# An encoder trunk on one core: the second sum of a seven-product pair in its own tile, one unit's copies dealt out, and two constants rebuilt later

## The chip, the cores and the metric

The kernel runs on one core of one Trainium2 chip. Its time is the device time of one execution, in microseconds. The core has a tensor engine (PE), a vector engine (DVE), a scalar engine (ACT), GpSimd (POOL) and SyncE (SP). Each works through its own queue of instructions in order and waits on semaphores; transfers are issued from the queues of SP, POOL and ACT.

## The reference

Two residual layers on x of 256 tokens by 2048 features, all in float32. The first layer's mixer is grouped-query attention, the second's a recurrent block; each is followed by a gated feed-forward layer.

```python
D_MODEL = 2048; SEQ = 256; DEPTH = 2
D_FF = 5632

def swiglu(h, w_gate, w_up, w_down):
    return (jax.nn.silu(h @ w_gate) * (h @ w_up)) @ w_down

def reference(x, ...):
    for i in range(DEPTH):
        h = rms_norm(x, norm_mix[i])
        mix = attention_mixer(h, ...) if i % N_MIXERS == 0 else recurrent_mixer(h, ...)
        x = x + mix
        x = x + swiglu(rms_norm(x, norm_ffn[i]), ffn_w_gate[i], ffn_w_up[i], ffn_w_down[i])
    return x
```

## The kernel before

**Products.** Every float32 operand is split in two parts that PE can multiply fast: hi, a cast of the value by ACT, and lo, the value less hi, by DVE (here called the correction). One product of a 128x128 block of x with 128x512 weights is three matmuls (`product`, L323, L324, L326): hi by hi, lo by hi, hi by lo.

**Feed-forward layer.** 5632 hidden features are eleven units of 512 (`unit`). A unit multiplies all of x (two token blocks) with 512 columns of the gate and 512 of the up matrix. The 2048 features of x are eight pairs of blocks, numbered 0 to 7. A pair comes in two forms:

- With eight products (`wide`): the gate half and the up half are loaded, 128x1024 each, cast by ACT (L145) and corrected by DVE (L146).
- With seven products (`load_seven`, after Strassen): the weights b11, b21, t1, b22 come in two landing buffers (raw), and further operands are formed: t1 = b11 + t1 (by DVE, L174, if the three loads before were of eight-product pairs, otherwise by an adding transfer on POOL, L176), then t2 = t1 + b22, t3 = t2 - b11, t4 = b21 + t2 (L169, DVE). Each is cast (L163 for the two whole buffers, L170 for t2, t3 and t4) and corrected (L164, L171). PE takes them in the order b11, b21, t1, b22, t2, t3, t4.

`SEVEN` and `FEWER` say which pairs have seven products: six of the eight (0, 1, 2, 4, 5, 6) in most units, fewer in the first three: 0, 5, 6 in the first, 4, 5, 6 in the second, 1, 4, 5, 6 in the third (the code's units 0, 1, 2).

At the end of a unit, from its pair 7 on, DVE and ACT put the products together (`sums`, L769 to L773, and L791, L794), apply SiLU, multiply gate by up (L795), and turn the result from tokens to features: DVE transposes 32x32 blocks (L408), sixteen copies put them in place (L416, in four moves of four), and L801 and L802 split the result into hi and lo. If `beside` is set, the four moves are put into a list (`tail`), and the next unit's seven-product pairs take one each; the last is followed by L801 and L802. `beside` is set for all units but the first and the last. The first unit's sixteen copies are issued at once, on ACT.

After the third unit come down projections, two groups behind each unit.

**Buffers.** Loads land in eight buffers during a feed-forward layer (five of a standing pool, three of the layer's own pool), and hi and lo go to seven pairs of buffers; t2's hi and lo have two of their own. t2 was written over b22, in the second landing buffer, so it had to wait until b22 was cast and corrected, and the buffer was held until t2 was corrected.

**Order.** PE executes in the order in which the program is written. A scheduler sets the order on the other engines, by times that it estimates and by rules in the code: `behind` keeps all casts in their written order on ACT, and all corrections and sums in theirs on DVE.

**Before the recurrent layer.** When the first feed-forward layer's pool is closed, the recurrent layer's pool ("rp") opens in its place. The norm's factors, one a token, are needed as a row (`Norm.spread`, due 26 steps later): DVE multiplies ident, the unit matrix, by them (dg, L492), PE multiplies ones by dg (L493), ACT copies the row (L495), and the convolution uses it (L842). ones and ident stand in a pool that lasts for the whole program; ident is loaded at the start, from in_cn_dram.

Of the kernel before, what the change touches and what calls it, by code (L numbers as in the profile page):

```python
# [12 lines left out]
F32 = mybir.dt.float32  # L13
F32R = mybir.dt.float32r
AF = mybir.ActivationFunctionType
ALU = mybir.AluOpType
AX = mybir.AxisListType

P = 128
S = 256  # L20
# [7 lines left out]
PARTS = [8, 8, 8, 8, 12]  # L28
UNIT = 4
SEVEN = (0, 1, 2, 4, 5, 6)  # L30
FEWER = {0: (0, 5, 6), 1: (4, 5, 6), 2: (1, 4, 5, 6)}
HALF = 8
CHUNK = HALF * P
WIDE = 512
# [40 lines left out]
def trunk(ctx, tc, w, out):  # L75
# [17 lines left out]
    def tmp(tag, shape=(P, S), dt=F32, bufs=2):  # L93
        pl = tp if tag in COMMON else scope[-1]
        return pl.tile(list(shape), dt, tag=tag, name=nm(tag), bufs=bufs)
# [58 lines left out]
    def load_seven(srcs, soon):  # L154
        raw = [landing([P, 2, WIDE]) for _ in range(2)]
        for r, src in zip(raw, srcs):
            sync.dma_start(out=r, in_=src)
        (b11, b21), (t1, b22) = ([r[:, j, :] for j in range(2)] for r in raw)
        got = {}

        def two(src, names):
            hi, lo = parts([P, 2, WIDE])
            behind("cast", act.copy(hi, src))  # L163
            behind("rest", dve.tensor_tensor(lo, src, hi[:].bitcast(F32), ALU.subtract))  # L164
            for j, name in enumerate(names):
                got[name] = hi[:, j, :], lo[:, j, :]

        def combine(o, x, y, op, hi, lo):
            behind("rest", dve.tensor_tensor(o, x, y, op))  # L169
            behind("cast", act.copy(hi, o))  # L170
            return lambda: behind("rest", dve.tensor_tensor(lo, o, hi.bitcast(F32), ALU.subtract))  # L171

        if soon:
            behind("rest", dve.tensor_tensor(t1, b11, t1, ALU.add))  # L174
        else:
            pool.dma_start(out=t1, in_=b11, accum_op=ALU.add)  # L176
        two(raw[0], ("b11", "b21"))
        two(raw[1], ("t1", "b22"))
        if tail:
            tail.pop(0)()  # L180
        one = [tmp(t, (P, WIDE), F32R) for t in ("ohi", "olo")]
        hi, lo = parts([P, 2, WIDE])
        got["t2"] = tuple(one)
        got["t3"], got["t4"] = ((hi[:, j, :], lo[:, j, :]) for j in range(2))
        t2 = b22
        rests = [
            combine(t2, t1, b22, ALU.add, *got["t2"]),
            combine(b11, t2, b11, ALU.subtract, *got["t3"]),
            combine(b21, t2, b21, ALU.add, *got["t4"]),
        ]  # L190
        while parted:
            follow(parted.pop(), newest["cast"])
        for rest in rests:
            rest()
        return got
# [71 lines left out]
    def later(delay, fn):  # L267
        waiting.append((clock[0] + delay, fn))
# [113 lines left out]


    x_tm = cst.tile([P, 2, D], F32, tag="x", name="x")
    ident = cst.tile([P, P], F32, tag="ident", name="ident")
    pk = cst.tile([P, PKW], F32, tag="pk", name="pk")
    at = ctx.enter_context(ExitStack())
    ap = at.enter_context(tc.tile_pool(name="ap", bufs=2))
    scope.append(ap)
    xq = [ap.tile([P, 4, S], F32, tag=f"xq{k}", name=f"xq{k}", bufs=1) for k in range(KT // 4)]  # L390
    cn = ap.tile([P, 2 * S], F32, tag="cn", name="cn", bufs=1)
    ones = cst.tile([P, P], F32, tag="ones", name="ones")
    act.dma_start(out=pk[:, :PK0], in_=w["pk"][:, :PK0])
    pool.memset(ones, 1.0)
    idle = ps_m.tile([P, P], F32, tag="pm", name=nm("pm"))
# [354 lines left out]
    def ffn(norm, nxt):  # L750
# [60 lines left out]
        ends = np.cumsum(PARTS) // UNIT  # L811
        for what, i in ffn_plan():
            if what == "unit":
                hid[int(np.searchsorted(ends, i, "right"))] += unit(FEWER.get(i, SEVEN), 0 < i < ends[-1] - 1, (act,) if i < ends[-1] - 1 else (act, dve), i < ends[0])
            else:
                for a, acc in enumerate(wide_project(hid[i[0]], PARTS[i[0]], bank)):
                    t = tmp("form", (P, WIDE))
# [14 lines left out]

    rt = ctx.enter_context(ExitStack())
    scope.append(rt.enter_context(tc.tile_pool(name="rp", bufs=2)))
    later(SPREAD, nr.spread)

    def conv_branch(ct, bank, first=False):
# [205 lines left out]
```

## Time and profile before

| | |
|---|---|
| time, median of 3 runs | 1952.84 us (1952.83 to 1952.92) |
| the profiled execution's own time | 1952.89 us |
| its span, first to last instruction | 1951.1 us |
| granted clock of PE | 1.000 |
| busy: PE / DVE / ACT / POOL | 1938.0 / 1768.6 / 1448.3 / 401.3 us |
| first feed-forward layer | about 266 to 950 us of the span |
| recurrent layer begins | about 950 us |

A row of the timeline gives start and length in us, engine, line, operation, out<-in and shape; in brackets the idle time of the engine before it and what ended it. Matmuls overlap, so their lengths (0.39) are longer than the distance of their starts (0.227). L123 is line 123 of the kernel before; in the changed kernel some lines are moved by one to three.

### The profile page before, as it was taken

To read this page: it belongs to the slowest core of one execution; us is meant where nothing else is said; L and a number is where in the kernel's file an instruction comes from. 1 tells how busy PE (TensorE), PEld (TensorE's weight loads), DVE (VectorE), ACT (ScalarE), POOL (GpSimd) and SP (SyncE) were. 2 spreads that over 40 slices of the span, in tenths; PEclk is the share of its full clock that TensorE was granted. 3 is DMA by queue.
4 is the path that set the end of the run, shared out by engine and by line. 5 is a ranking of instruction groups with operands and counts; after the bars stand their busy time and mean duration, and the time that the engine had idled before them with its cause. 6 is when DMAs were issued, how large, how long until landed. Compare 5 with 4: busy or idle time off the path is not lost.

```text
span 1951.1 us, 27630 instructions
## 1 busy us (share of the span) xinstructions
PE 1938.0 (99%) x9224; PEld 1624.0 (83%) x9224; DVE 1768.6 (91%) x2417; ACT 1448.3 (74%) x2358; POOL 401.3 (21%) x497
## 2 busy tenths in 40 slices
PE   9999999999999999999999999999999999999999
PEld 8898888788888888888899998887888888888887
DVE  7878698999999999998799997898999999999993
ACT  7677686777777777777698887866778776787772
POOL 0442250011101111010465450520101111011100
PEclk9999999999999999999999999999999999999999
DMA  8434746698878978787365556555878888788872
GB/s 328 156 127 152 248 158 197 196 272 236 248 233 243 262 240 246 235 244 246 126 223 188 189 164 245 175 194 174 253 236 248 245 248 253 231 246 251 246 257 86
DMA packets 131727, 426.42 MB, mean 219 GB/s; under 512 B 14720, under 2 KB 14976, under 8 KB 131584
## 3 DMA queue, kind: packets, MB, share of 16 engines
q1 hardware_dynamic: 108944, 383.21, 58.0%
q0 software_dynamic: 22496, 41.43, 11.9%
q8 instruction: 72, 1.18, 0.2%
q14 instruction: 71, 0.58, 0.1%
q10 hardware_dynamic: 144, 0.02, 0.0%
HBM read 382.13 MB, written 2.10 MB: 197 GB/s over the span
## 4 chain that ended last, share of the span: by engine, by line
PE 92%; DVE 4%; ACT 1%; issue 1%; DMA 1%; POOL 0%; SPq 0%; ACTq 0%; DVEq 0%; POOLq 0%
PE acc L326 14%; PE acc L323 14%; PE acc L324 14%; PE pm L326 11%; PE pm L323 11%; PE pm L324 11%; PE acc L294 8%; PE acc L292 4%; PE pm L306 1%; PE pm L307 1%; PE pm L305 1%; DVE lo L146 1%; ACT hi L145 1%; DVE lo L164 0%; DMA raw<-in_w_in_dram 0%
## 5 line engine op out<-in xcount | busy, mean ns | idle before, releaser
L146 DVE TENSOR_TENSOR lo<-raw,hi 128x1024 fp32r<-128x1024 f32 (+1 forms) x474 | 574.5, 1240 | 77.1 <-ACT hi L145 75.3
L145 ACT CAST hi<-raw 128x1024 fp32r<-128x1024 f32 (+1 forms) x474 | 478.4, 1045 | 116.5 <-PE acc L324 72.1
L326 PE MATMUL acc<-lo,xg 128*128 128x512 f32 x744 | 290.9, 391 | 2.0 <-DVE lo L146 1.8
L323 PE MATMUL acc<-hi,xg 128*128 128x512 f32 x744 | 290.0, 390 | 0.0
L324 PE MATMUL acc<-hi,xg 128*128 128x512 f32 x744 | 289.6, 389 | 0.0
L164 DVE TENSOR_TENSOR lo<-raw,hi 128x1024 fp32r<-128x1024 f32 x232 | 275.0, 1217 | 6.5 <-ACT hi L163 3.8
L294 PE MATMUL acc<-xg,hi 128*128 128x512 f32 x832 | 271.7, 397 | 0.6 <-ACT hi L145 0.6
L163 ACT CAST hi<-raw 128x1024 fp32r<-128x1024 f32 x232 | 234.6, 1048 | 41.0 <-issue 14.4
L176 POOL DMA_DIRECT2D raw<-raw x90 | 77.7, 863 | 903.9 <-DVE raw L174 369.5
L323 PE MATMUL pm<-hi,act 128*128 128x512 f32 x512 | 199.2, 389 | 0.0
L324 PE MATMUL pm<-hi,act 128*128 128x512 f32 x512 | 199.2, 389 | 0.0
L326 PE MATMUL pm<-lo,act 128*128 128x512 f32 x512 | 199.2, 389 | 0.0
L416 ACT COPY two<-one 32x256 f32<-32x256 f32 x420 | 169.7, 404 | 24.7 <-DVE one L408 16.5
L292 PEld LDWEIGHTS acc<-xg,lo 128*128 128x128 f32 x832 | 156.3, 188 | 35.4 <-DVE lo L146 2.8
L323 PE MATMUL acc<-hi,act 128*128 128x512 f32 x448 | 174.9, 390 | 0.4 <-DVE two L794 0.4
L326 PE MATMUL acc<-lo,act 128*128 128x512 f32 x448 | 174.4, 389 | 0.0
L324 PE MATMUL acc<-hi,act 128*128 128x512 f32 x448 | 174.4, 389 | 0.0
L292 PE MATMUL acc<-xg,lo 128*128 128x256 f32 x832 | 171.8, 281 | 1.2 <-DVE lo L146 1.2
L326 PEld LDWEIGHTS acc<-lo,xg 128*128 128x128 f32 x744 | 139.7, 188 | 34.1 <-DVE lo L146 5.4
L324 PEld LDWEIGHTS acc<-hi,xg 128*128 128x128 f32 x744 | 139.7, 188 | 29.2
L323 PEld LDWEIGHTS acc<-hi,xg 128*128 128x128 f32 x744 | 139.7, 188 | 28.6
L170 ACT CAST hi<-raw 128x512 fp32r<-128x512 f32 x232 | 137.1, 622 | 32.8 <-DVE raw L169 31.8
(221 smaller groups left out, 3852.1 us busy)
## 6 DMA issues: line engine op xcount, KB each, us to landing
raw<-in_w_gate_dram SPq DMA_DIRECT2D x176, 512.0 KB, 4.6
raw<-in_w_up_dram SPq DMA_DIRECT2D x176, 512.0 KB, 5.5
raw<-in_w_down_dram SPq DMA_DIRECT2D x176, 512.0 KB, 4.4
raw<-in_w_in_dram SPq DMA_DIRECT2D x64, 512.0 KB, 4.4
raw<-raw POOLq DMA_DIRECT2D x90, 256.0 KB, 5.8
raw<-in_w_q_dram SPq DMA_DIRECT2D x32, 512.0 KB, 3.8
raw<-in_w_o_dram SPq DMA_DIRECT2D x32, 512.0 KB, 4.2
x<-form POOLq DMA_DIRECT2D x64, 256.0 KB, 6.7
```

Source lines behind the costliest of these rows:

```text
L145: behind("cast", act.copy(hi[:, sl], raw[:, sl]))
L146: behind("rest", dve.tensor_tensor(lo[:, sl], raw[:, sl], hi[:, sl].bitcast(F32), ALU.subtract))
L163: behind("cast", act.copy(hi, src))
L164: behind("rest", dve.tensor_tensor(lo, src, hi[:].bitcast(F32), ALU.subtract))
L170: behind("cast", act.copy(hi, o))
L176: pool.dma_start(out=t1, in_=b11, accum_op=ALU.add)
L292: pe.matmul(acc[:, S:], w, xs[k][:, :S], start=False, stop=stop)
L294: pe.matmul(acc, w, xs[k], start=(k == 0), stop=stop)
L323: pe.matmul(o, xh, wh, start=start, stop=False)
L324: pe.matmul(o, xl, wh, start=False, stop=False)
L326: pe.matmul(o, xh, wl, start=False, stop=stop)
L416: m = (eng.copy if eng is act else eng.tensor_copy)(to[:, :, :, i, :], of[:, :, :, j, :])
```

## The change

1. t2 gets a tile of its own (`sum`, one buffer). Its sum is issued ahead of the casting and correcting of the second landing buffer on DVE, and its cast ahead of the move of copies that the pair takes from the list. t3 and t4 are formed, cast and corrected as before, their casts behind the copies.
2. `beside` is set for the first unit too: its copies are dealt out over the second unit's seven-product pairs, which are four now.
3. The second unit's pairs with seven products become 2, 4, 5, 6 (three before), the third's 2, 4, 5, 6 in place of 1, 4, 5, 6.
4. ones and ident leave the pool that lasts for the whole program. They are built in the attention layer's pool, and again in the recurrent layer's pool, by a memset and a transfer on POOL.

```diff
-FEWER = {0: (0, 5, 6), 1: (4, 5, 6), 2: (1, 4, 5, 6)}
+FEWER = {0: (0, 5, 6), 1: (2, 4, 5, 6), 2: (2, 4, 5, 6)}
...
         two(raw[0], ("b11", "b21"))
+        got["t2"] = hi, lo = tuple(tmp(t, (P, WIDE), F32R) for t in ("ohi", "olo"))
+        t2 = tmp("sum", (P, WIDE), bufs=1)
+        behind("rest", dve.tensor_tensor(t2, t1, b22, ALU.add))
         two(raw[1], ("t1", "b22"))
+        behind("cast", act.copy(hi, t2))
         if tail:
             tail.pop(0)()
-        one = [tmp(t, (P, WIDE), F32R) for t in ("ohi", "olo")]
-        hi, lo = parts([P, 2, WIDE])
-        got["t2"] = tuple(one)
-        got["t3"], got["t4"] = ((hi[:, j, :], lo[:, j, :]) for j in range(2))
-        t2 = b22
+        both = parts([P, 2, WIDE])
+        got["t3"], got["t4"] = (tuple(t[:, j, :] for t in both) for j in range(2))
         rests = [
-            combine(t2, t1, b22, ALU.add, *got["t2"]),
+            lambda: behind("rest", dve.tensor_tensor(lo, t2, hi[:].bitcast(F32), ALU.subtract)),
             combine(b11, t2, b11, ALU.subtract, *got["t3"]),
             combine(b21, t2, b21, ALU.add, *got["t4"]),
         ]
...
-    ident = cst.tile([P, P], F32, tag="ident", name="ident")
...
-    ones = cst.tile([P, P], F32, tag="ones", name="ones")
+    ones, ident = (ap.tile([P, P], F32, tag=t, name=t, bufs=1) for t in ("ones", "ident"))
...
-                hid[...] += unit(FEWER.get(i, SEVEN), 0 < i < ends[-1] - 1, ...)
+                hid[...] += unit(FEWER.get(i, SEVEN), i < ends[-1] - 1, ...)
...
     scope.append(rt.enter_context(tc.tile_pool(name="rp", bufs=2)))
+    ones, ident = (tmp(t, (P, P), bufs=1) for t in ("ones", "ident"))
+    pool.memset(ones, 1.0)
+    pool.dma_start(out=ident, in_=w["cn"][:, 2 * S :])
     later(SPREAD, nr.spread)
```

How the order on the engines changes, at the three places that the prediction speaks of. First, ACT in the second unit of the first feed-forward layer, from the cast of the first seven-product pair's first buffer on (L163 casts a buffer, L416 are the first unit's copies, L170 and in the changed kernel L182 cast t2, t3 and t4). Before, pair 4:

```order
L163 CAST hi_3735<-raw_3730 128x1024
L163 CAST hi_3739<-raw_3731 128x1024
L416 COPY two_3221<-one_3556 32x8x32 x16
L170 CAST ohi_3743<-raw_3731 128x512
L170 CAST hi_3745<-raw_3730 128x512 x2
L163 CAST hi_3782<-raw_3777 128x1024
```

And now, pair 2:

```order
L163 CAST hi_3656<-raw_3644 128x1024
L182 CAST ohi_3652<-sum_3654 128x512
L416 COPY two_3221<-one_3559 32x8x32 x4
L170 CAST hi_3665<-raw_3643 128x512 x2
L145 CAST hi_3696<-raw_3695 128x1024
L145 CAST hi_3714<-raw_3713 128x1024
L163 CAST hi_3736<-raw_3731 128x1024
```

Sixteen copies stood ahead of the casts of t2, t3 and t4; now four stand behind t2's and ahead of t3's and t4's, and four more in each of the next three pairs.

Second, DVE in one seven-product pair without L174. Before, pair 6 of the second unit:

```order
L164 TENSOR_TENSOR lo_3830<-raw_3824,hi_3829 128x1024
L164 TENSOR_TENSOR lo_3834<-raw_3825,hi_3833 128x1024
L169 TENSOR_TENSOR raw_3825<-raw_3825 128x512
L169 TENSOR_TENSOR raw_3824<-raw_3825,raw_3824 128x512 x2
L171 TENSOR_TENSOR olo_3838<-raw_3825,ohi_3837 128x512
L171 TENSOR_TENSOR lo_3840<-raw_3824,hi_3839 128x512 x2
```

And now, where the first unit's L802 falls into the same pair:

```order
L164 TENSOR_TENSOR lo_3841<-raw_3835,hi_3840 128x1024
L180 TENSOR_TENSOR sum_3846<-raw_3836 128x512
L164 TENSOR_TENSOR lo_3849<-raw_3836,hi_3848 128x1024
L169 TENSOR_TENSOR raw_3835<-sum_3846,raw_3835 128x512 x2
L188 TENSOR_TENSOR olo_3845<-sum_3846,ohi_3844 128x512
L171 TENSOR_TENSOR lo_3860<-raw_3835,hi_3859 128x512
L802 TENSOR_TENSOR act_3558<-two_3221,act_3558 128x4x256
L171 TENSOR_TENSOR lo_3860<-raw_3835,hi_3859 128x512
```

The t2 sum moved ahead of the second buffer's correction; L802 stands ahead of t4's correction.

Third, the beginning of the recurrent layer, on POOL and on DVE. Before, POOL:

```order
L416 COPY two_9340<-one_9339 32x8x32 x4
L840 MEMSET cb_9479 128x2
L841 MEMSET cb_9479 128x2
L840 MEMSET cb_9494 128x2
L841 MEMSET cb_9494 128x2
L871 DMA graw_9508<-in_w_gates_dram 128x512
```

And now:

```order
L416 COPY two_9410<-one_9409 32x8x32 x4
L836 MEMSET ones_9444 128x128
L837 DMA ident_9445<-in_cn_dram 128x128
L843 MEMSET cb_9553 128x2
L844 MEMSET cb_9553 128x2
L843 MEMSET cb_9568 128x2
L844 MEMSET cb_9568 128x2
L874 DMA graw_9582<-in_w_gates_dram 128x512
```

DVE before, from the last scaling of the normed x (L436) on:

```order
L436 SCALAR_TENSOR_TENSOR xg_9367<-two_9340,pk,xg_9367 128x256
L492 TENSOR_SCALAR dg_9456<-ident,nr_9332 128x128 x2
L146 TENSOR_TENSOR lo_9533<-raw_9531,hi_9532 128x1024
L146 TENSOR_TENSOR lo_9555<-raw_9553,hi_9554 128x1024
L146 TENSOR_TENSOR lo_9593<-raw_9591,hi_9592 128x1024
```

And now:

```order
L436 SCALAR_TENSOR_TENSOR xg_9437<-two_9410,pk,xg_9437 128x256
L146 TENSOR_TENSOR lo_9607<-raw_9605,hi_9606 128x1024
L146 TENSOR_TENSOR lo_9629<-raw_9627,hi_9628 128x1024
L492 TENSOR_SCALAR dg_9530<-ident_9445,nr_9402 128x128 x2
L146 TENSOR_TENSOR lo_9667<-raw_9665,hi_9666 128x1024
```

On POOL the memset of ones and the transfer of ident came in front; on DVE two corrections moved ahead of L492, which now reads the ident of that transfer. PE's L493 stands where it stood.

More of the change, by code (lines that the diff above doesn't have):

```diff
@@ L813, in ffn @@
             if what == "unit":
-                hid[int(np.searchsorted(ends, i, "right"))] += unit(FEWER.get(i, SEVEN), 0 < i < ends[-1] - 1, (act,) if i < ends[-1] - 1 else (act, dve), i < ends[0])
+                hid[int(np.searchsorted(ends, i, "right"))] += unit(FEWER.get(i, SEVEN), i < ends[-1] - 1, (act,) if i < ends[-1] - 1 else (act, dve), i < ends[0])
             else:
```

## The prediction

> **What bounds the kernel now.** I read the page first, then the waits of the tensor engine, then its instructions in order of time where the waits fall, and last the vector and scalar engines' instructions in the same stretches.
>
> ```profile
> span 1951.1 us, 27630 instructions
> PE 1938.0 (99%) x9224; PEld 1624.0 (83%) x9224; DVE 1768.6 (91%) x2417; ACT 1448.3 (74%) x2358; POOL 401.3 (21%) x497
> PE pm L323 <- ACT ohi L170: 2.4, 2, 1.2
> PE acc L326 <- DVE lo L146: 1.8, 3, 0.8
> PE acc L292 <- DVE lo L146: 1.2, 3, 0.6
> PE pm L493 <- DVE dg L492: 0.7, 1, 0.7
> ```
>
> PE sets the end: it is idle for 13 us in all. (Columns of the last four rows: us in total, times, longest.) "Busy" hides what it loses, though, because matmuls overlap. The starts show more:
>
> ```profile
> 329.63 0.39 PE L323 MATMUL pm<-hi,xg 128*128 128x512 f32 x1
> 349.52 0.39 PE L326 MATMUL acc<-lo,xg 128*128 128x512 f32 x1
> 349.75 0.39 PE L323 MATMUL acc<-hi,xg 128*128 128x512 f32 x1
> 349.98 0.39 PE L324 MATMUL acc<-hi,xg 128*128 128x512 f32 x1
> 351.20 0.50 PE L326 MATMUL acc<-lo,xg 128*128 128x512 f32 x1 [0.84 <-DVE lo L146]
> 358.86 0.39 PE L326 MATMUL acc<-lo,fh 128*128 128x512 f32 x1
> 360.42 0.50 PE L323 MATMUL pm<-ohi,fh 128*128 128x512 f32 x1 [1.18 <-ACT ohi L170]
> 307.90:393.00 85.10, 82.94 (x358) 66.32 (x357) 79.03 (x97) 59.24 (x91) 3.44 (x4) 1.00 0.63 203
> 393.00:870.00 477.00, 477.00 (x2107) 395.08 (x2106) 462.68 (x562) 355.98 (x519) 62.56 (x72) 1.00 0.83 246
> ```
>
> Unhindered, a matmul starts every 0.227 us, so a product (three) takes 0.68, a pair of eight products 5.44 and a pair of seven 4.76. The last two rows are stretches (length, then busy time and count of PE, PEld, DVE, ACT, POOL). From 393 to 870, the fourth to the eleventh unit of the first feed-forward layer, 2107 matmuls fill 477 us at 0.226 each: nothing is lost there, while DVE has 14 us of idle time. From 307.9 to 393, the second and third unit, 358 matmuls should take 81.2 us and took 85.1: 3.9 us are lost. The loss repeats in the second layer (the rows above count the ohi wait twice, once a layer). So of the places that the change touches three can move the end: these two units, in both layers, and the spread at 959 us, below.
>
> What makes DVE late in those two units:
>
> ```profile
> 320.76 6.64 ACT L416 COPY two<-one 32x256 f32<-32x256 f32 x16 [1.11 <-DVE one L408]
> 328.08 0.69 DVE L171 TENSOR_TENSOR olo<-raw,ohi 128x512 fp32r<-128x512 f32 x1 [4.19 <-ACT ohi L170]
> 308.68 5.76 DVE L146 TENSOR_TENSOR lo<-raw,hi 128x1024 fp32r<-128x1024 f32 x5
> 314.35 1.21 DVE L795 TENSOR_TENSOR two<-two,one 128x1024 f32<-128x1024 f32 x1
> 337.22 2.35 DVE L164 TENSOR_TENSOR lo<-raw,hi 128x1024 fp32r<-128x1024 f32 x2
> 341.55 0.69 DVE L171 TENSOR_TENSOR olo<-raw,ohi 128x512 fp32r<-128x512 f32 x1
> 343.35 1.22 DVE L146 TENSOR_TENSOR lo<-raw,hi 128x1024 fp32r<-128x1024 f32 x1
> 349.93 1.22 DVE L146 TENSOR_TENSOR lo<-raw,hi 128x1024 fp32r<-128x1024 f32 x1
> ```
>
> The first unit's sixteen copies stand in ACT's queue ahead of the cast of t2, and DVE idles 4.19 us for that cast. Then it runs without a rest. A seven-product pair takes it 6.13 us (337.22 to 343.35), more than PE's 4.76; an eight-product pair takes two instructions of 1.134 (five between 308.68 and 314.35), less than PE's 5.44. DVE lives on what it gains in the eight-product pairs.
>
> **The change part by part.** *One more seven-product pair* in the second unit of each layer: PE saves three matmuls, 3 x 0.227 = 0.68 us a layer. DVE pays 6.13 - 2.27 = 3.86 more there. In the third unit the number stays four; pair 4 no longer follows two eight-product pairs, so its t1 leaves DVE (0.60 by the three instructions between 341.55 and 343.35) for a transfer on POOL.
>
> ```profile
> raw<-raw POOLq DMA_DIRECT2D x90, 256.0 KB, 5.8
> 374.65 1.05 ACT L163 CAST hi<-raw 128x1024 fp32r<-128x1024 f32 x1 [0.88 <-DMA raw<-raw]
> ```
>
> I cost that transfer at nothing: the eight landing buffers let pair 4 be loaded when the unit's first half is corrected, three pairs ahead, which covers 5.8 us. Uncovered it would cost some 0.9, as at 374.65.
>
> *The first unit's copies dealt out, four to a pair.* DVE's idle 4.19 goes. In its place comes a shorter wait in each pair with copies. The new order on ACT is cast t2, four copies, casts t3 and t4, then the next pair's first cast:
>
> ```profile
> 358.07 1.65 ACT L416 COPY two<-one 32x256 f32<-32x256 f32 x4 [3.37 <-DVE one L408]
> 359.75 0.62 ACT L170 CAST ohi<-raw 128x512 fp32r<-128x512 f32 x1
> 360.28 1.14 ACT L170 CAST hi<-raw 128x512 fp32r<-128x512 f32 x2
> 361.32 3.89 ACT L145 CAST hi<-raw 128x1024 fp32r<-128x1024 f32 x4
> ```
>
> From the end of the t2 sum that is 0.53 + 1.68 + 2 x 0.52 + 1.05 and some 0.1 of hand-over, 4.4 us, until DVE may begin the next pair. DVE itself has 1.14 + 5 x 0.60 = 4.14 to do. It waits 0.3 a pair.
>
> *t2 in a tile of its own.* The instruction count is the same. The sum may now stand ahead of the second correction, and neither it nor t3 waits for its predecessor's write. A pair is 2 x 1.134 + 6 x 0.60 = 5.87 instead of 6.13, and with the 0.3 about 6.2 where copies are dealt. So the two edits cancel in a unit's steady part: from 393 to 870 I cost them at nothing, covered by DVE's 14 us of idle time, some 1.9 a unit; four waits of 0.3 less six gains of 0.26 do not use that up.
>
> Added up for the second unit: its second half is corrected from 308.68, as before. Three halves take DVE to 312.1. Pair 2 (t1 0.6, two corrections of 1.134, t2, t3 and t4 and three corrections of 0.6, the first unit's product and transpose, two more instructions of the large size, and 0.7 of waiting for the copies) takes 9.4, to 321.5. Pair 3 takes 0.3 + 2.3, to 324.1. Pairs 4 to 6 take 5.9 + 6.2 + 6.3, and the first unit's L802, which now falls inside pair 6 and waits for ACT's L801, 1.4: the last correction ends at 344.1. PE began the unit at 307.9 (329.63, its first product of pair 4, less four pairs of 5.44) and would want that tile after three pairs of 5.44, three of 4.76, six products and two matmuls, at 343.0. So 1.1 is lost. The next half is 1.14 behind while PE takes 0.68: another 0.45. Then come the unit's sums; before, from 343.35 to the end of the half at 349.93, they took 7.8 against PE's 5.44 and two matmuls: 1.15 more. The third unit runs in the same pattern and loses 1.6 up to 393. Together 4.3, against 3.9 before: the freed 4.19 us of DVE went into the extra pair. With the 0.68 the layer gains 0.25, both layers 0.5. Bounds: were the 0.3 a pair and the wait for L801 absent, each unit would lose 1 us less, 5 us of gain for both layers; were a pair to take 0.3 longer still, four pairs in each of four units lose 4.8.
>
> *ident and ones rebuilt for the recurrent layer.* This is the largest term.
>
> ```profile
> 957.48 1.69 DVE L436 SCALAR_TENSOR_TENSOR xg<-two,pk,xg 128x256 fp32r<-128x256 f32 x4
> 959.20 0.48 DVE L492 TENSOR_SCALAR dg<-ident,nr 128x128 f32<-128x128 f32 x2
> 958.68 0.40 PE L294 MATMUL acc<-xg,hi 128*128 128x512 f32 x1
> 959.80 0.68 PE L493 MATMUL pm<-dg,ones 128*128 128x128 f32 x4 [0.73 <-DVE dg L492]
> 959.36 0.16 POOL L840 MEMSET cb<- 128x2 f32 x1 [3.86 <-PE acc L294]
> 959.98 2.19 POOL L871 DMA_DIRECT2D graw<-in_w_gates_dram  x4 [0.42 <-issue]
> 963.66 1.39 POOL L872 CAST ghi<-graw 128x512 fp32r<-128x512 f32 x1 [1.49 <-DMA graw<-in_w_gates_dram]
> 973.14 1.15 DVE lo L146
> 974.34 0.50 PE acc L292 x2
> out_dram<-x SPq DMA_DIRECT2D x8, 256.0 KB, 2.0
> ```
>
> The new tiles lie in a pool that takes over the memory of the feed-forward pool. The first instruction of POOL that writes there now is the memset at 959.36, 0.2 us after DVE's last L436 has read that memory (957.48 + 1.69). The new memset of ones takes that place, and the transfer of ident the place of the first graw, at 959.98. That graw had landed 3.68 us later. I take 3.3 for ident, with a quarter of the bytes: 963.3. Bounds: nothing less than 2.0, the median of the quickest kind of transfer on the page (the stores of the output), and 5.8, the median of POOL's own raw. L492 cannot start before; PE's L493 follows its start by 0.6, so it begins at 963.9 instead of 959.8. PE keeps its written order and nothing may pass L493: 4.1 us are lost (2.8 to 6.6). Behind L492 in DVE's queue stand the third half's correction and the convolution, all for PE's work after L493, so they shift with it. Two halves now stand ahead of L492, so DVE comes out of the stall some 2 us ahead of where it was against PE, and the wait at 974.34 (0.5) should go. The four graw transfers start 0.6 later, hidden by PE's delay. Net 3.6.
>
> [...]
>
> *The rest.* Startup only changes the pools of ident and ones. Sum against the profiled execution's own 1952.89: -0.5 + 3.6 = +3.1, so 1956.0; the median of the runs is 0.05 lower: 1955.9.
>
> **The rivals.** *Faster: the dealt copies free DVE.* If DVE gets through pairs with copies without the 0.3 and without waiting for L801, the loss in units two and three shrinks. All of it is 3.9 + 0.68 = 4.6 a layer, 9.2 for both; less 3.6 gives 1947.2. For it speaks that ACT has idle time (59 busy of 85). Against it: the end of each of these units has 7.8 us of DVE work against 5.9 of PE's, whatever precedes it. It decides for "faster" from a gain of 3.8 a layer on; half of it gives 1951.8.
>
> *The clock falls during the stall.*
>
> ```profile
> 0.99 4.63 PE L397 MATMUL pm<-ones 128*128 128x128 f32 x20 [0.99 <-POOL ones L394]
> ```
>
> The first twenty instructions of PE, 128 columns each, start 0.22 apart (4.63 us for twenty); the four of L493, of the same size, 0.11 apart (0.68 us with the length of the last). So PE runs at half speed after a long rest, for at least 4.6 us. At the spread PE would rest from 959.1 to 963.9, 4.8 us; the trace has no such rest inside the program, the longest being 1.2, after which the speed stays. If it falls, 4.6 us at half speed cost 2.3: 1958.2. [...]
>
> *Slower: ACT becomes the bound in pairs with copies.* If every such pair in units two and three takes 0.3 to 0.6 longer than I reckon, 16 of them make 4.8 to 9.6: 1960.7 to 1965.5. For it: with copies, ACT's chain is already the longer one. Against it: its members are all in the rows above.
>
> *The spread does not wait:* ident lands in time. Then the change gives 1952.3. Against it stands the memset at 959.36.
>
> **How the numbers follow.** Forecast 0.47 (own range 1953.5 to 1957.8), copies free DVE 0.20, clock falls 0.18, ACT the bound 0.10, no wait 0.05. The time is the forecast's, 1955.9. The range of 8 in 10 is 1949.0 to 1960.0. A measurement tells 0.2%, 3.9 us, from no change: faster is below 1948.9, slower above 1956.7. Faster: half of the first rival and a little, 0.11. Slower: the clock, ACT, and a third of the forecast's own range, 0.43. Within: 0.46.
>
> **What would show it.** L493 waits for L492 some 4 us longer, L492 for the transfer of ident, at about 959. The second unit has three matmuls fewer, and units two and three lose about 4 us as now; the wait of PE for ohi is gone and stands as waits for lo at the units' ends instead. DVE's wait of 4.19 for ohi is gone. From 393 to 870 PE still loses nothing. I am wrong if ident's landing does not end PE's longest wait, if the two units lose under 2 us or over 6, or if PE starts to wait after 393.

## The result, and the profile after

| | before | after |
|---|---|---|
| time, median (runs) | 1952.84 us (4) | 1962.39 us (4; 1962.11 to 1967.45) |
| ratio of the times | | 1.0056, 95% interval 1.0038 to 1.0073 |
| the profiled execution's own time | 1952.89 us | 1962.11 us |
| granted clock of PE | 1.000 | 0.999 |

The change makes the kernel slower, by 0.56%; 1955.9 us was predicted, with a range up to 1960.0. First the page of the changed kernel, and PE's longest waits (us in total, times, longest):

```profile
span 1960.3 us, 27643 instructions
PE 1939.2 (99%) x9218; PEld 1622.7 (83%) x9218; DVE 1760.6 (90%) x2427; ACT 1447.0 (74%) x2364; POOL 410.3 (21%) x503
PE pm L493 <- DVE dg L492: 3.4, 1, 3.4
PE acc L327 <- DVE lo L146: 3.2, 7, 0.9
PE acc L327 <- DVE lo L171: 2.4, 4, 0.6
PE acc L324 <- DVE two L794: 1.1, 2, 0.5
PE pm L324 <- ACT fh L474: 1.0, 1, 1.0
PE pm L325 <- DVE fl L475: 0.5, 1, 0.5
```

The six matmuls fewer are there (9218 for 9224), and the span grew by 9.2 us. Two rows are new in kind: the waits for fh and fl, the two parts of what the norm makes of x, which the prediction does not mention. Next, three stretches of the kernel before and the same three of the changed kernel, from matmul to matmul: the second and third unit of layer one, the steady part behind them, the second and third unit of layer two (length, then busy time and count of PE, PEld, DVE, ACT, POOL).

```profile
308.10:393.07 84.97, 82.81 (x357) 66.20 (x356) 78.91 (x96) 59.11 (x91) 3.44 (x4) 1.00 0.63 204
393.07:870.21 477.14, 477.14 (x2107) 395.21 (x2105) 462.82 (x563) 356.12 (x519) 62.56 (x72) 1.00 0.83 246
1305.09:1390.07 84.98, 82.78 (x358) 66.20 (x356) 78.85 (x96) 58.42 (x90) 3.45 (x4) 1.00 0.63 204
```

```profile
310.33:395.70 85.37, 82.53 (x355) 65.62 (x353) 81.71 (x101) 60.98 (x94) 5.15 (x6) 1.00 0.69 210
395.70:873.15 477.45, 477.45 (x2107) 394.93 (x2105) 455.02 (x561) 353.26 (x517) 62.67 (x72) 1.00 0.83 246
1311.97:1398.93 86.96, 83.01 (x354) 65.48 (x353) 83.57 (x104) 62.52 (x97) 5.16 (x6) 1.00 0.67 206
```

With three matmuls fewer, the two units take 0.40 us longer in layer one and 1.98 in layer two. The steady part is within 0.3. In layer two the stretch already starts 6.9 us late. PE's instructions where it loses time, in order, show the rest (start, length; in brackets the idle time before):

```profile
298.90 0.39 PE L327 MATMUL acc<-lo,xg 128*128 128x512 f32 x1
300.33 0.50 PE L324 MATMUL pm<-hi,fh 128*128 128x512 f32 x1 [1.05 <-ACT fh L474]
301.37 0.50 PE L325 MATMUL pm<-hi,fl 128*128 128x512 f32 x1 [0.54 <-DVE fl L475]
...
345.29 0.50 PE L324 MATMUL acc<-hi,xg 128*128 128x512 f32 x1 [0.24 <-ACT hi L170]
346.63 0.51 PE L327 MATMUL acc<-lo,xg 128*128 128x512 f32 x1 [0.61 <-DVE lo L171]
347.77 0.50 PE L327 MATMUL acc<-lo,xg 128*128 128x512 f32 x1 [0.16 <-DVE lo L146]
354.35 0.50 PE L327 MATMUL acc<-lo,xg 128*128 128x512 f32 x1 [0.81 <-DVE lo L146]
...
961.93 0.40 PE L295 MATMUL acc<-xg,hi 128*128 128x512 f32 x1
965.76 0.68 PE L493 MATMUL pm<-dg,ones 128*128 128x128 f32 x4 [3.43 <-DVE dg L492]
966.92 1.05 PE L295 MATMUL acc<-xg,hi 128*128 128x512 f32 x2
...
1311.97 0.39 PE L325 MATMUL acc<-hi,xg 128*128 128x512 f32 x1
1313.30 0.49 PE L327 MATMUL acc<-lo,xg 128*128 128x512 f32 x1 [0.95 <-DVE lo L146]
```

A matmul that follows another 1.43 us after its start instead of 0.227 loses 1.2 us. Counted so, the 9.2 us lie in five places: at the spread 3.6, in the first unit 2.0 in layer one (at 299 and 300) and 1.1 in layer two (at 1312, the end of that unit's work), in the second and third unit 0.4 and 0.9 (the 1.98 less those 1.1), at the end of each feed-forward layer 0.35 (the wait for L794), in the steady part 0.3. That makes 9.0.

### The profile page after: what moved, and what is told of

It reads as the page before. It is cut to its first block, busy times and chain, and to the rows that moved or that the text cites. A ratio compares the mean times of both kernels' runs of the same rounds, so it can differ in the third digit from the quotient of the medians.

```text
span 1960.3 us, 27643 instructions
## 1 busy us (share of the span) xinstructions
PE 1939.2 (99%) x9218; PEld 1622.7 (83%) x9218; DVE 1760.6 (90%) x2427; ACT 1447.0 (74%) x2364; POOL 410.3 (21%) x503
## 4 chain that ended last, share of the span: by engine, by line
PE 85%; DVE 7%; ACT 3%; issue 3%; POOL 1%; DMA 1%; SPq 0%; ACTq 0%; DVEq 0%; POOLq 0%
PE acc L327 12%; PE acc L324 12%; PE acc L325 12%; PE pm L325 10%; PE pm L324 10%; PE pm L327 10%; PE acc L295 9%; PE acc L293 4%; DVE lo L146 2%; PE pm L307 1%; PE pm L308 1%; PE pm L306 1%; ACT two L416 1%; DVE lo L164 1%; POOL form L472 1%
## 5 line engine op out<-in xcount | busy, mean ns | idle before, releaser
L327 PE MATMUL acc<-lo,xg 128*128 128x512 f32 x732 | 286.6, 392 | 5.7 <-DVE lo L146 3.2
L164 DVE TENSOR_TENSOR lo<-raw,hi 128x1024 fp32r<-128x1024 f32 x236 | 287.8, 1219 | 4.4 <-ACT hi L163 4.3
L324 PE MATMUL acc<-hi,xg 128*128 128x512 f32 x732 | 285.8, 390 | 1.0 <-ACT hi L170 1.0
L325 PE MATMUL acc<-hi,xg 128*128 128x512 f32 x732 | 284.9, 389 | 0.0
L295 PE MATMUL acc<-xg,hi 128*128 128x512 f32 x832 | 272.6, 399 | 1.4 <-DVE xg L436 0.9
L163 ACT CAST hi<-raw 128x1024 fp32r<-128x1024 f32 x236 | 238.5, 1048 | 42.3 <-issue 24.1
L171 DVE TENSOR_TENSOR lo<-raw,hi 128x512 fp32r<-128x512 f32 x236 | 155.1, 691 | 40.0 <-ACT hi L170 35.7
L416 ACT COPY two<-one 32x256 f32<-32x256 f32 x420 | 169.5, 404 | 23.1 <-DVE one L408 16.2
L170 ACT CAST hi<-raw 128x512 fp32r<-128x512 f32 x236 | 138.7, 620 | 40.2 <-DVE raw L169 37.4
L324 PEld LDWEIGHTS acc<-hi,xg 128*128 128x128 f32 x732 | 137.4, 188 | 30.3 <-ACT hi L170 2.2
```

What stands on the lines that cost most here:

```text
L295: pe.matmul(acc, w, xs[k], start=(k == 0), stop=stop)
L324: pe.matmul(o, xh, wh, start=start, stop=False)
L325: pe.matmul(o, xl, wh, start=False, stop=False)
L327: pe.matmul(o, xh, wl, start=False, stop=stop)
L416: m = (eng.copy if eng is act else eng.tensor_copy)(to[:, :, :, i, :], of[:, :, :, j, :])
```

## The experiments

Each was timed in three rounds beside the kernel before on the same chip (parts_joined in five); "ratio" is to that kernel, with the 95% interval. The kernel before lay between 1952.66 and 1953.15 us in these timings, so a difference of half a microsecond from the changed kernel, which was timed apart from them, says nothing. What a profile lost at a place is counted by starts, as above.

**Edit 4 alone.**

```diff
 kernel before
-    ident = cst.tile([P, P], F32, tag="ident", name="ident")
...
-    ones = cst.tile([P, P], F32, tag="ones", name="ones")
+    ones, ident = (ap.tile([P, P], F32, tag=t, name=t, bufs=1) for t in ("ones", "ident"))
...
+    ones, ident = (tmp(t, (P, P), bufs=1) for t in ("ones", "ident"))
+    pool.memset(ones, 1.0)
+    pool.dma_start(out=ident, in_=w["cn"][:, 2 * S :])
```

> The kernel before with edit 4 alone: ones and ident leave the lasting pool and are rebuilt in the recurrent layer's pool. Theory A (the loss at the spread belongs to this edit alone): PE waits about 3 us more for L492 at the recurrent layer's start, the granted clock falls to a half for 3.4 us behind that wait, and the wait of 0.5 at 974 goes; time 1952.9 + 3.6 = 1956.5 us, nothing else in the trace moves. Rival B (the spread is late because DVE comes to it late from the other edits): at most 1 us lost there, 1952.9 to 1953.9 us, and no fall of the clock.

Measured: 1956.94 us (before 1953.15), ratio 1.0020 (1.0011 to 1.0030): 3.8 us. DVE, POOL and PE of this kernel at the spread:

```profile
960.57 2.36 DVE L146 TENSOR_TENSOR lo<-raw,hi 128x1024 fp32r<-128x1024 f32 x2 [0.45 <-ACT hi L145]
963.13 0.48 DVE L491 TENSOR_SCALAR dg<-ident,nr 128x128 f32<-128x128 f32 x2 [0.20 <-DMA ident<-in_cn_dram]
960.32 0.20 POOL L835 MEMSET ones<- 128x128 f32 x1 [3.87 <-PE acc L294]
960.86 0.57 POOL L836 DMA_DIRECT2D ident<-in_cn_dram  x1 [0.33 <-issue]
963.52 0.68 PE L492 MATMUL pm<-dg,ones 128*128 128x128 f32 x4 [3.49 <-DVE dg L491]
```

PE waits 3.5 us, for dg, and dg for the landing of ident, 2.27 us after its issue; the two corrections ahead of it on DVE end 0.2 earlier. So theory A stands on the wait. On the rest it missed in this profile: the clock does not fall at the spread (below), and PE loses only 2.1 us more there than in the kernel before (3.65 at L492, where the kernel before lost 0.90 and, around 974, another 0.64). What else the time contains stands elsewhere: 1.1 more in the first 25 us of the program, 0.7 at 1010 us and 0.4 at 1171, where the kernel before loses nothing. (The first 25 us differ by up to 1.7 us between the profiles, by 1.1 between parts_joined and less_and_joined below, which are the same there.)

**Edits 2 and 3 alone, t2 over b22 as before.**

```diff
 kernel before
-FEWER = {0: (0, 5, 6), 1: (4, 5, 6), 2: (1, 4, 5, 6)}
+FEWER = {0: (0, 5, 6), 1: (2, 4, 5, 6), 2: (2, 4, 5, 6)}
...
-    ... unit(FEWER.get(i, SEVEN), 0 < i < ends[-1] - 1, ...)
+    ... unit(FEWER.get(i, SEVEN), i < ends[-1] - 1, ...)
```

> The kernel before with edits 2 and 3 alone: the first unit's copies dealt out and the new pairs in units 2 and 3, t2 written over b22 as before, ones and ident untouched. Theory A (DVE is what these two units wait for, whatever precedes it): 6 matmuls fewer (-1.4), the two units lose 4.3 to 5.7 us a layer in place of 4.3, the first unit nothing: 1951.5 to 1954.5 us. Rival C (it is the tile of t2 and its order that cost the units their gain): the units lose under 3 us a layer, 1949 us or less. Rival D (new pairs and dealt copies also make the first unit lose): PE waits at 298 us as in the changed kernel, 1955 us or more.

Measured: 1950.06 us (before 1953.15), ratio 0.9986 (0.9977 to 0.9996). These two edits make the kernel faster by 3.1 us, more than theory A allows: the two units take 83.58 us in layer one where the kernel before takes 84.97 and the changed kernel 85.37. The time falls between theory A and rival C, and so does the loss of the two units, 3.4 us a layer (C: under 3). But C's point stands: what cost the units this gain is edit 1 on top of edits 2 and 3. DVE of this kernel, two pairs of the second unit:

```profile
323.95 2.35 DVE L164 TENSOR_TENSOR lo<-raw,hi 128x1024 fp32r<-128x1024 f32 x2
330.09 2.35 DVE L164 TENSOR_TENSOR lo<-raw,hi 128x1024 fp32r<-128x1024 f32 x2
```

A pair takes 6.14 us, and DVE has no rest. The same in the changed kernel:

```profile
326.28 1.22 DVE L164 TENSOR_TENSOR lo<-raw,hi 128x1024 fp32r<-128x1024 f32 x1
332.58 1.23 DVE L164 TENSOR_TENSOR lo<-raw,hi 128x1024 fp32r<-128x1024 f32 x1 [0.18 <-ACT hi L163]
338.89 1.23 DVE L164 TENSOR_TENSOR lo<-raw,hi 128x1024 fp32r<-128x1024 f32 x1 [0.18 <-ACT hi L163]
```

Here it takes 6.30, and DVE waits for ACT.

**Edits 1 and 4, the first three units as before.**

> The kernel before with edits 1 and 4: t2 in a tile of its own and the two constants rebuilt (without the latter the tile does not fit), the pairs and copies of the first three units as before. Theory A (the new loss in the first unit comes from edit 1, which puts the last steps of the norm behind the casts of t2, t3 and t4 on ACT): PE waits at 298 us for fh and fl as in the changed kernel, 2.2 us; in the second layer ACT's order is nearer to that of before, so 0 to 1.2; with 3.6 at the spread 1958.5 to 1960.5 us. Rival D (that loss comes from the new pairs and the dealt copies): 1956.5 us, no wait in the first unit.

Measured: 1959.33 us (before 1953.15), ratio 1.0034 (1.0021 to 1.0047). PE waits for fh and fl at 299 and 300 us as in the changed kernel (1.2 and 0.8 lost), in layer two not at all. Theory A holds for layer one: edit 1 brings the first unit's loss there, not the new pairs. The wait at 1312 us in layer two needs both: it stands neither here nor with edits 2 and 3 alone. Edit 1 by itself costs the second and third unit nothing: they take 84.72 us in layer one and 84.41 in layer two, 0.3 and 0.6 less than in the kernel before.

**The changed kernel, its first unit in the old form.**

```diff
 changed kernel, load_seven
+        if lead[0]:
+            two(raw[1], ("t1", "b22"))
...
+            t2 = b22
...
+        else:
...
```

lead[0] is set in the first unit of a layer; its branch is the code of the kernel before, the other that of the changed one.

> The changed kernel, but the first unit of each layer keeps t2 over b22 and its old order; from the second unit on as in the changed kernel. Theory A (edit 1's order in the first unit costs 2.2 in layer one and 1.2 in layer two): the waits for fh and fl at 298 us and for lo at 1312 go, 1962.1 - 3.4 = 1958.7 us; with layer two left, 1959.9. Rival E (PE, once ahead, loses the same at the next bound, units 2 and 3): these lose 2 us a layer more than now and the time stays at 1961 to 1962 us.

Measured: 1957.76 us (before 1953.15), ratio 1.0024 (1.0013 to 1.0034), 4.6 less than the changed kernel. The waits for fh, fl and the one at 1312 are gone, as theory A has it; it forecast 3.4 less. In the profile the first units account for 3.1 us; the clock does not fall at the spread here (1.00 from 957.4 to 967.6 us), which is worth 1.5 more, and a wait at 1010 us takes 1.3 back. So 4.6 is not the first unit's share alone. The mechanism in layer one is read from ACT. In the changed kernel, end of the first unit:

```profile
293.73 0.62 ACT L182 CAST ohi<-sum 128x512 fp32r<-128x512 f32 x1 [0.85 <-DVE sum L180]
294.26 0.90 ACT L466 ACTIVATE form<-two,pk 128x256 f32<-128x256 f32 x2
299.66 0.62 ACT L474 CAST fh<-form 128x512 fp32r<-128x512 f32 x1 [1.41 <-POOL form L472]
```

And in the kernel before:

```profile
287.25 0.62 ACT L170 CAST ohi<-raw 128x512 fp32r<-128x512 f32 x1 [0.49 <-DVE raw L169]
287.78 0.90 ACT L466 ACTIVATE form<-two,pk 128x256 f32<-128x256 f32 x2
292.46 0.62 ACT L474 CAST fh<-form 128x512 fp32r<-128x512 f32 x1 [0.48 <-POOL form L472]
```

L466 makes the norm's last form, POOL (L472) combines it, ACT casts it to fh, and pair 6 needs fh and fl. The scheduler, which orders everything that `behind` does not tie, now puts L466 behind the cast of pair 6's t2 (before, behind that of pair 5's), 6.5 us later; PE was idle 1.05 us for fh and 0.54 for fl. In first_unit_old ACT's order there is again that of the kernel before, in layer one row for row. No run moved L466 alone. In layer two of the changed kernel fh's cast stands ahead of pair 6's cast of t2, and ACT stands still for POOL:

```profile
1301.17 0.62 ACT L474 CAST fh<-form 128x512 fp32r<-128x512 f32 x1 [5.25 <-POOL form L472]
```

In the kernel before this wait is 1.40 us. The corrections behind it come late up to the end of the unit, where PE waits at 1312.

**The copies ahead of t2's cast.**

```diff
 changed kernel, load_seven
+        if tail:
+            tail.pop(0)()
         behind("cast", act.copy(hi, t2))
-        if tail:
-            tail.pop(0)()
```

> The changed kernel with two lines exchanged: the four copies of a pair stand on ACT ahead of the cast of t2 instead of behind it; all else as in the changed kernel. Theory F (in units 2 and 3 DVE waits for the casts of t3 and of the next pair because the copies stand in front of them; a pair takes DVE 6.30 us where it takes 6.13 with t2 in place): a pair with copies falls to 5.9, the two units lose 2 to 3.6 us a layer in place of 5.4 to 5.7, time 1962.1 less 4 to 7 = 1955 to 1958 us. Rival G (what costs the units is the tile's sum or its single buffer, wherever the copies stand): pairs stay at 6.3 us and the time at 1961 to 1963 us.

Measured: 1958.26 us (before 1952.66), ratio 1.0028 (1.0017 to 1.0040), 4.1 less than the changed kernel. Theory F holds for the units; the time lies 0.3 above its range. DVE of this kernel:

```profile
328.04 1.22 DVE L164 TENSOR_TENSOR lo<-raw,hi 128x1024 fp32r<-128x1024 f32 x1
333.92 1.22 DVE L164 TENSOR_TENSOR lo<-raw,hi 128x1024 fp32r<-128x1024 f32 x1
```

A pair takes 5.88 us, without waits. The two units lose 2.1 us less in layer one and 1.9 in layer two. The ends of the feed-forward layers are back at 0.51 from 0.85 too. Together that is more than the profile gained (3.2): behind the first unit's waits for fh and fl the clock fell to a half in this profile (0.50 from 301.85 to 305.27 us), and 3.8 us were lost there in place of 2.0.

**Less work for DVE in units 2 and 3.** Is DVE the bound there, as I had it? Without t4's correction (light[0] is set in units 2 and 3):

```diff
 changed kernel, load_seven
+        if light[0]:
+            rests.pop()
+            got["t4"] = got["t4"][0], got["t4"][0]
```

> The changed kernel without the correction of t4 in the pairs of units 2 and 3 (lo of t4 is left out there, PE multiplies with its hi twice, so these products are less exact): 8 instructions of 0.6 us less for DVE in each layer, nothing else left out, PE's work unchanged. Theory P (DVE is the bound of these two units): the 5.4 to 5.7 us that PE loses there fall to under 1.5 a layer, time 1962.4 - 8 = 1954.4 us (1953 to 1956). Rival Q (ACT's order or the loads hold these units): the loss stays over 4 us a layer, 1960 us or more.

Measured: 1961.74 us (before 1952.94), ratio 1.0043 (1.0028 to 1.0058): no gain that can be told from the changed kernel. In the profile the two units take 0.8 and 0.6 us less, and 0.6 of it is lost again at the end of the first feed-forward layer; theory P asked for 4 a layer. It falls, by these rows:

```profile
326.22 1.22 DVE L165 TENSOR_TENSOR lo<-raw,hi 128x1024 fp32r<-128x1024 f32 x1
332.53 1.23 DVE L165 TENSOR_TENSOR lo<-raw,hi 128x1024 fp32r<-128x1024 f32 x1 [0.78 <-ACT hi L164]
338.83 1.23 DVE L165 TENSOR_TENSOR lo<-raw,hi 128x1024 fp32r<-128x1024 f32 x1 [0.78 <-ACT hi L164]
```

The pair stays at 6.30, and DVE's wait grew from 0.18 to 0.78, by just the 0.6 that was left out. So in the changed kernel a chain that closes on itself from pair to pair (a round) sets the pace: correction, t2's sum, its cast, the copies, the casts of t3 and t4, the next pair's cast, its correction. With the copies ahead of t2's cast they fall into the time in which ACT waits for that sum anyway, and the round is broken.

**Keeping ident.**

```diff
 changed kernel
+    keep = cst.tile([P, P], mybir.dt.bfloat16, tag="keep", name="keep")
...
+        act.copy(keep, ident)
...
-    ones, ident = (tmp(t, (P, P), bufs=1) for t in ("ones", "ident"))
-    pool.dma_start(out=ident, in_=w["cn"][:, 2 * S :])
+    ones, ident = tmp("ones", (P, P), bufs=1), keep
```

> The changed kernel, but ident is cast once, at the end of the attention layer, to a two-byte tile that lasts for the whole program; only ones is rebuilt, by the memset. L492 stands on DVE directly behind L436 again. Theory A (what L493 waits for is the landing of ident, and the two corrections that were put ahead of L492): PE waits 0.7 us there, as before the change, the clock does not fall, the wait of 0.5 to 0.9 at 974 is back; time 1962.1 - 3.6 = 1958.5 us, half a microsecond less where the fall of the clock cost something. Rival H (the memset of ones, which waits for DVE's last L436, is enough to hold PE): the wait stays over 2 us and the time over 1961 us.

Measured: 1961.18 us (before 1952.66), ratio 1.0043 (1.0028 to 1.0059). PE waits 0.6 at the spread, now for the memset of ones (rival H falls), but the time is only 1.2 less, not 3.6. The profile shows two places that lose more than in the changed kernel. One is the clock, in the first unit. PE there, and two windows (behind the five engines' busy times stands the clock):

```profile
300.58 0.50 PE L324 MATMUL pm<-hi,fh 128*128 128x512 f32 x1 [1.16 <-ACT fh L475]
301.62 0.55 PE L325 MATMUL pm<-hi,fl 128*128 128x512 f32 x1 [0.53 <-DVE fl L476]
303.25 0.63 PE L327 MATMUL acc<-lo,fh 128*128 128x512 f32 x1
298.51:301.92 3.41, 1.72 (x7) 0.90 (x6) 3.41 (x6) 2.01 (x4) 1.29 (x2) 1.00 0.36 121
301.92:305.33 3.41, 3.41 (x9) 2.65 (x8) 1.28 (x5) 3.41 (x6) 0.00 (x0) 0.50 0.93 262
```

Here the waits for fh and fl (7 matmuls in 3.41 us, two of them under way at its start) were followed by 3.41 us at half clock, and the first unit lost 4.3 us, not 2.0. This explains the profile and not the median: the profiled execution is the slowest of four (1962.07), and two of the others, at 1961.02 and 1961.14, show a granted clock of 1.000, where a fall of 3.41 us within the span would leave 0.999. The other place is the recurrent layer: a wait for L382 at 1010 us and one at 1172, 1.2 us lost in both, which neither the kernel before nor the changed one has. What else keeps the executions without a fall from gaining 3.6 stays open.

**Ident kept, and the first unit in its old form.**

> The changed kernel with two of the repairs: ident kept in two bytes and the first unit in its old form. Keeping ident alone took PE's loss at the spread from 5.3 to 1.0 us and the time by only 1.2 us, since in its profile the clock fell to a half for 3.4 us behind the first unit's waits (4.3 us lost there in place of 2.2). Theory M (that fall, set off by the first unit's waits, ate the gain): without these waits the clock stays up, and against the run with the first unit alone in its old form (1957.8 us) 3.3 us go: 1954.5 us, or up to 1955.5 with a wait left at about 1010 us. Rival N (keeping ident is worth 1.2 us wherever it is done, since the recurrent layer loses the rest again): 1956.5 us or more.

Measured: 1956.19 us (before 1952.94), ratio 1.0018 (1.0008 to 1.0028): 1.6 less than with the first unit alone. The clock does not fall in its profile (the fastest of ten executions, 1955.08), but the waits at 1007 and 1168 are there again (0.80 and 0.34). It lies between M and N.

**PE kept busy at the spread.**

```diff
 changed kernel, Norm.spread of the recurrent layer
+            if self.g[0] == "norm_mix":
+                for i in range(24):
+                    pe.matmul(pst[:, S:], self.xs[0][:, :P], self.xs[0][:, :S], start=True, stop=True)
```

> The changed kernel with 24 extra matmuls of 256 columns (about 2.9 us) on PE directly ahead of L493, into a part of its bank that nothing reads, so that PE works through most of its wait for L492; L493 begins no later. Theory J (the rest of 3.4 us makes the granted clock fall to a half for 3.4 us, which costs 1.4 us): no fall of the clock at 966 in any profile, 1.4 us less: 1960.7 us. [...]

Measured: 1961.21 us (before 1952.66), ratio 1.0045 (1.0032 to 1.0059). The time alone does not decide on J: it lies 0.5 above J's and 1.2 below the changed kernel's, with an interval of 2.6 us either way. The profile speaks for J: no fall of the clock (mean granted clock 1.000), no new wait at 1009, and a span of 1959.2, 1.1 less than the changed kernel's.

**All three repairs.**

> The changed kernel with the three repairs together: ident kept in two bytes, t2 in its own tile only from the second unit on, and the copies ahead of the cast of t2. Theory A with F (each place loses by itself and nothing else is behind it): 1962.1 less 3.6, 4.4 and 4 to 7 = 1947.1 to 1950.1 us, faster than the kernel before by 3 to 6 us. Rival E (with one bound gone the next one takes the gain): 1951 us or more.

Measured: 1949.55 us (before 1952.66), ratio 0.9984 (0.9975 to 0.9993): faster than both kernels, by 3.1 and 12.8 us, as theory A with F forecast, and not to be told from edits 2 and 3 alone. PE waits 0.6 at the spread, the two units take 83.39 us in layer one, and the recurrent layer has no wait at 1009.

**Two of them, edit 4 as in the change.**

> The changed kernel with the first unit in its old form and the copies ahead of the cast of t2; ident and ones rebuilt as in the changed kernel. If the places add up: the run with all three repairs (1949.6 us) plus what edit 4 cost alone (3.8) = 1953.4 us, no different from before by what can be measured. Rival E (one place's loss hides another's): 1951 us or less, or 1956 us or more.

Measured: 1953.54 us (before 1952.94), ratio 1.0002 (0.9992 to 1.0011): the places add up; edit 4 costs 4.0 here, and the other three edits, with the two repairs, pay for it. Undone together, the first unit's order and the copies' place are worth 8.9 us against the changed kernel; undone singly they gave 4.6 and 4.1.

**All three, with less work for DVE.**

> The run with all three repairs, without the correction of t4 in the pairs of units 2 and 3 (its lo is left out, PE takes hi twice). In the changed kernel the same cut gave nothing: DVE's wait for the next pair's cast grew from 0.18 to 0.78 and a pair stayed at 6.30 us, so there the round of t2's sum, its cast, the copies, the casts of t3, t4 and of the next pair and its correction sets the pace. Theory R (with the copies ahead of t2's cast that round is broken and DVE itself is the bound): a pair falls from 5.88 to 5.3 us, PE's loss in the two units from 3.3 to under 1.8 us a layer, time 1949.6 - 3.5 = 1946 us. Rival S (another round through ACT sets the pace there as well): pairs stay at 5.88, 1949 us or more.

Measured: 1949.41 us (before 1952.83), ratio 0.9982 (0.9973 to 0.9992). Theory R misses; rival S holds in the time and, but for 0.07 us, in the pair. DVE:

```profile
325.40 1.22 DVE L166 TENSOR_TENSOR lo<-raw,hi 128x1024 fp32r<-128x1024 f32 x1
331.21 1.23 DVE L166 TENSOR_TENSOR lo<-raw,hi 128x1024 fp32r<-128x1024 f32 x1 [0.44 <-ACT hi L165]
```

A pair falls from 5.88 to 5.81 only, and DVE waits for ACT again, 0.44 us a pair: behind DVE stands at once another round through ACT. The two units still lose 1.1 to 1.2 us less a layer, since DVE does less at their ends; the recurrent layer lost 1.1 of it again, in waits at 1005 and 1166, and the start of the program 1.1.

**What stays open.** A wait at about 1009 us, 0.8 us lost, stands in three kernels with ident kept: ident_kept, ident_and_first and less_and_joined. Behind the spread these three have one and the same order on DVE, ACT and POOL; parts_joined, without the wait, has another, on DVE and ACT that of the kernel before. So the scheduler's order is the likely cause; no run changed it alone. Waits of 1.1 and 0.5 us at that place in first_unit_old and const_alone, and one of some 0.35 at about 1170 in most of the kernels, may have the same cause or not. Whether a wait at the spread brings half clock also differs from profile to profile: with 3.4 to 3.5 us of idle time it did in the changed kernel, t2_and_const, copies_first, less_for_dve and edit4_left, in the last for 6.8 us, and did not in const_alone and first_unit_old.

## Why the prediction was wrong

| place | predicted | in the profile | by the runs |
|---|---|---|---|
| spread (edit 4) | +3.6 | +3.6 | +3.8 (const_alone; 2.1 of it at the spread in its profile) |
| units 2 and 3, both layers | -0.5 | +1.3 | edits 2, 3: -3.1; copies behind t2's cast: +4.1 |
| first units | 0 | +3.1 | +4.6 (undone in first_unit_old; 3.1 of it there in the profiles) |
| ends of the feed-forward layers, steady part | 0 | +1.0 | part of the 4.1 |

The runs' shares, 3.8 - 3.1 + 4.1 + 4.6, make 9.4 of the 9.55 measured. That they come so close is in part luck: each has an interval of about 2 us either way, and, as said at each run, 3.8, 4.6 and 4.1 hold differences of the clock and of the recurrent layer beside their own place. The profile's column is the surer one for the places.

- **The step that failed: "of the places that the change touches three can move the end".** The first unit is not among the three, and "The rest" names the startup alone. It was costed at nothing without a reason: none of the edits to its pairs seemed to move work. But edit 1 also changes load_seven in the first unit, where the norm's forms run beside it, and the scheduler moved L466 behind a cast, which cost 2.0 us in layer one; in layer two another order cost 1.1, as the rows have it through ACT's wait for POOL. That is a third of the loss, and half of what the forecast missed. None of the prediction's signs of being wrong looks at the first unit. For layer one the order of the changed kernel on ACT showed it: L466 stood behind pair 5's casts of t3 and t4 and pair 6's two L163 and L182, all of which had stood behind it.
- **"The two edits cancel" failed in units two and three, where DVE has no idle time to cover the difference.** Here I compared the pair in its own tile (6.2 with copies) with the pair before (6.13) and held the copies' place for given. The pair measured 6.30. The round of 4.4 us through ACT that I added up was right, and it, not DVE's work, set the pace: less_for_dve shows it. With t2 in place the copies cost nothing (6.14), with the tile and the copies ahead 5.88. So rival "ACT becomes the bound" was there in kind, and held too unlikely at 0.10. That its times, 1960.7 to 1965.5, hold the measured one is luck: a pair took 0.1 longer than reckoned, not 0.3 to 0.6, and the rest of the loss came from elsewhere.
- **The units' waits came where they were forecast.** Second unit: 1.1, 0.45 and 1.15 forecast; the starts of the rows above give 0.5 + 0.8, 0.33 and 0.97. Third: 1.6 and 1.64. The last correction of pair 6 was to end 35.4 us behind the unit's first, and ended after 35.7. The sum was compared wrongly: 4.3 of named waits against 3.9 of all that was lost. Counted alike, from the lengths above at 0.227 a matmul, layer one loses 4.2 before (84.97 for 356; the counts of the stretches, the prediction's 358 too, also hold matmuls that were under way at the start) and 5.2 after (85.37 for 353). Two of the steps to 4.3 also do not come out as written: 324.1, 18.4 and 1.4 make 343.9 and not 344.1, and 7.8 less 5.44 and two matmuls is 1.9, of which 0.45 was counted before, so 1.45 and not 1.15; the two nearly cancel.
- **The spread: the sum of 3.6 was right by luck, its terms were not.** The transfer of ident took 2.27 us from issue to use (const_alone), not 3.3: the row of graw, with its 3.68, was the wrong neighbour. L493 started 2.7 us later (3.83 behind the last L295, 1.12 before), not 4.1. The clock fell as in the rival, but for 3.41 us, which cost 1.4: two L295 take 1.05 in place of 0.63. (The rival's 4.6 us are the slow start of PE's first matmuls; that a long rest brings as much was not shown: ahead of those matmuls the trace has 0.99 us of idle time.) So a wait that was 1.4 shorter than forecast and a fall that the sum left out made up for each other; in const_alone's profile, without the fall, the spread lost 2.1. The wait of 0.5 at 974 went as forecast.
- **Right as predicted:** three matmuls fewer a layer; PE's waits for ohi gone, and of DVE's 23.4 us of them all but one of 1.8; nothing lost from 393 to 870 beyond 0.3; L492 behind ident's landing (const_alone).

## What to carry to other kernels

Where a scheduler sets the order, an edit to a helper acts wherever the helper runs: go through the changed order at every place, and above all where other work on the same engines has a deadline, before costing a place at nothing. A piece of work that is dealt out belongs into a gap in which its engine waits anyway (here ahead of t2's cast); behind it, the same four copies became part of the round that sets the pace. Before calling an engine the bound, take work off it: if only its wait grows, the round through another engine is the bound.

## What the runs showed of the hardware that was not expected

The clock fell without one long rest before it. With ident kept, the longest rest of PE before the fall was 1.16 us, and PE ran 7 matmuls, in part or whole, in the 3.41 us ahead of it; in copies_first the longest was 1.06 us, and PE ran 8. At the spread of the changed kernel the rest was 3.43 us. Inside the program the fall lasts 3.41 us in the changed kernel, copies_first and ident_kept, and twice that in edit4_left. The falls of one profile lie whole numbers of 3.413 us apart: those of the changed kernel, from 966.52 us and, behind the last matmul, from 1959.80, 291 times that; those of copies_first, from 301.85 and 964.04, 194 times. Two stretches of const_alone of about that length that no fall followed, at a wait of 3.49 us:

```profile
958.40:961.80 3.40, 1.63 (x10) 1.17 (x8) 2.91 (x6) 3.40 (x7) 1.15 (x7) 1.00 0.00 0
961.80:965.20 3.40, 1.68 (x11) 1.58 (x12) 2.75 (x4) 1.26 (x3) 1.94 (x4) 1.00 0.63 172
```

The longer wait was split between two stretches of 10 and 11 matmuls, and the clock stayed up (1.00 up to 968.6 us). So much the same wait cost more in one kernel than in another: against the kernel before, 2.1 us more were lost at the spread in const_alone (wait 3.49), 3.6 in the changed kernel (3.43), 4.8 in edit4_left. And two short waits within one stretch, 1.16 and 0.53 us in ident_kept, were followed by 3.41 us at half clock as the one of 3.43 was. The counts of matmuls don't tell the stretches with a fall behind them from the others, since these stretches hold shorter matmuls too. An estimate from all fourteen profiles does better: count 0.227 us for a matmul of 512 columns and shorter ones in proportion, and lay the stretches 3.413 us apart, back from the fall with which every profile ends. Behind the first 12 us, the stretches ahead of the seven falls inside the program are idle for 63% (copies_first), 64% (ident_kept) and 80 to 99% (the five at the spread; 86% in the changed kernel); of all other stretches at full clock up to PE's last matmul none is idle for more than 60%, the two of const_alone above for 58 and 60. Why the clock falls, no run shows.
